# Eight experts on one core: six output stores moved into the load queue, a third output buffer, and a narrower last weight piece

## The chip, the cores and the metric

The kernel runs on one core of one Trainium2 chip. The metric is device time in microseconds for one execution of the whole program; lower is better.

## The reference

Each of 8 experts has its own 256 tokens and its own two-layer network; all tensors are float32 in HBM.

```python
n_experts, capacity, hidden, expert_hidden = 8, 256, 512, 2048
h = np.matmul(x, w1) + b1[:, np.newaxis, :]
h = np.maximum(h, 0)
out = np.matmul(h, w2) + b2[:, np.newaxis, :]
```

The weights are 4 MB per expert and per layer in float32. Every weight is used once, so 64 MB of weights have to come in from HBM for 8.6 GFLOP of matmuls.

## The kernel before

**Loads.** All weights and the tokens of experts 2 to 7 are loaded by DMAs that GpSimd issues, and they are cast from float32 to float16 on the way (`load_x`, `load_w1`, `load_w2`). All of them go into one DMA queue, called q0 in the profile; this text calls it the ring. `w1[e]` and `w2[e]` are one DMA of 2 MB (written) each. `w2[6]` is two DMAs of 1 MB. `w2[7]` is six pieces with a buffer each: rows 0 to 4, 4 to 8 and 8 to 12 of the 16 row blocks j (512 KB each), rows 12 to 14 (256 KB), and then rows 14 to 16 twice, once for the left and once for the right half of the 512 columns (128 KB each). The text names them p0, p4, p8, p12, p14a and p14b.

**Compute.** `first_product(e)` makes h for one expert: for each of 16 blocks j four matmuls (line 110) into PSUM, then a ReLU with bias on ScalarE (line 117) into `hT`. In the middle of it the tokens of the next expert are transposed on TensorE (`transposes`, line 97). `second_product(e)` starts with one bias matmul per accumulator (line 151), runs 32 matmuls of 512 columns (line 163) and calls `store`. For expert 7 the 512 columns are two blocks of `HH` = 256, and the pieces of `w2[7]` are used in the order in which they were loaded; the last two pieces give 4 matmuls each.

**Stores.** `store` copies the accumulator of token block 0 with VectorE (line 130) and that of token block 1 with ScalarE (line 131) to SBUF. For experts 0 to 6 SyncE then issues one DMA of 512 KB (line 137), which runs in another queue, q1 in the profile. For expert 7 each column block is stored by two DMAs, one issued by SyncE (line 134) and one by ScalarE (line 135).

**Order.** The main loop has 11 steps s. Step s runs `first_product(s)` and then `second_product(s - 3)`, so expert 0's second product comes after expert 3's first. TensorE's and GpSimd's instructions keep the order in which the program writes them. `issue_until` lets GpSimd run ahead: at step s it issues loads up to `w1[s + 2]` and `w2[s - 1]`. The three buffers each of `w1` and `w2` make the issue wait for the product that last read the buffer.

Of the kernel before, what the change touches and what calls it, by code (L numbers as in the profile page):

```python
# [11 lines left out]
def kernel(  # L12
# [9 lines left out]
    nc = tc.nc  # L22
    fp32 = mybir.dt.float32
    fp16 = mybir.dt.float16
    E, T, H = x.shape
    M = w1.shape[2]
    P = 128
    nTB = T // P
    nKC = H // P
    nJ = M // P  # L30
    HH = H // 2
    LAG = 3
    nXF32 = 2

    def ordered(ins):
        return tc.keep_in_program_order(ins)

    singles = ctx.enter_context(tc.tile_pool(name="singles", bufs=1))
    w1_pool = ctx.enter_context(tc.tile_pool(name="w1", bufs=3))
    w2_pool = ctx.enter_context(tc.tile_pool(name="w2", bufs=3))  # L40
    w2t_pool = ctx.enter_context(tc.tile_pool(name="w2t", bufs=1))
    x_pool = ctx.enter_context(tc.tile_pool(name="xp", bufs=4))
    xT_pool = ctx.enter_context(tc.tile_pool(name="xTp", bufs=2))
    hT_pool = ctx.enter_context(tc.tile_pool(name="hT", bufs=LAG + 2))
    out_pool = ctx.enter_context(tc.tile_pool(name="outp", bufs=2))
    psum_x = ctx.enter_context(tc.tile_pool(name="psum_x", bufs=1, space=bass.MemoryType.PSUM))
    psum_h = ctx.enter_context(tc.tile_pool(name="psum_h", bufs=3, space=bass.MemoryType.PSUM))
    psum_o = ctx.enter_context(tc.tile_pool(name="psum_o", bufs=2, space=bass.MemoryType.PSUM))
# [10 lines left out]
    w1_sb = [None] * E  # L59
    w2_sb = [None] * E  # L60
    hT = [None] * E

    def load_x(e):
        x16[e] = x_pool.tile([P, nTB, H], fp16, tag="x16", name="x16")
        ordered(nc.gpsimd.dma_start(  # L65
            out=x16[e], in_=x[e].rearrange("(p tb) h -> p tb h", tb=nTB)
        ))
# [7 lines left out]
    def load_w2(e):  # L75
        src = w2[e].rearrange("(p j) h -> p j h", j=nJ)
        w2_sb[e] = []
        if e < E - 1:
            t = w2_pool.tile([P, nJ, H], fp16, tag="w2", name="w2sb")
            step = nJ if e < E - 2 else nJ // 2  # L80
            for lo in range(0, nJ, step):
                ordered(nc.gpsimd.dma_start(out=t[:, lo : lo + step, :], in_=src[:, lo : lo + step, :]))  # L82
                w2_sb[e].append((lo, lo + step, 0, H, t[:, lo : lo + step, :]))
            return
        for lo, hi, c0, c1 in (
            (0, 4, 0, H), (4, 8, 0, H), (8, 12, 0, H), (12, 14, 0, H),
            (14, 16, 0, HH), (14, 16, HH, H),
        ):
            t = w2t_pool.tile([P, hi - lo, c1 - c0], fp16, tag=f"w2_{lo}_{c0}", name=f"w2_{lo}_{c0}")
            ordered(nc.gpsimd.dma_start(out=t, in_=src[:, lo:hi, c0:c1]))  # L90
            w2_sb[e].append((lo, hi, c0, c1, t))

    def transposes(e):
        pt = psum_x.tile([P, nKC, T], fp16, tag="psx", name="psx")
        for kc in range(nKC):
            for tb in range(nTB):
                ordered(nc.tensor.transpose(  # L97
                    out=pt[:, kc, tb * P : (tb + 1) * P],
                    in_=x16[e][:, tb, :].rearrange("p (q kc) -> p q kc", kc=nKC)[:, :, kc],
                    identity=ident16,  # L100
                ))
        xT[e] = xT_pool.tile([P, nKC, T], fp16, tag="xT", name="xT")
        nc.vector.tensor_copy(out=xT[e], in_=pt)  # L103

    def first_product(e):
        hT[e] = hT_pool.tile([P, nJ, T], fp16, tag="hT", name="hT")
        for j in range(nJ):
            ph = psum_h.tile([P, T], fp32, tag="ph", name="ph")
            for kc in range(nKC):
                ordered(nc.tensor.matmul(  # L110
                    out=ph,
                    lhsT=w1_sb[e][:, kc, :].rearrange("p (q j) -> p q j", j=nJ)[:, :, j],
                    rhs=xT[e][:, kc, :],
                    start=(kc == 0),
                    stop=(kc == nKC - 1),
                ))
            nc.scalar.activation(  # L117
                out=hT[e][:, j, :],
                in_=ph,
                func=mybir.ActivationFunctionType.Relu,  # L120
                bias=b1T[:, j, e : e + 1],
                scale=1.0,
            )
            if j == nJ // 2 and e + 1 < E:
                transposes(e + 1)

    def store(e, po, c0, c1, split):
        w = c1 - c0
        out_sb = out_pool.tile([P, nTB, w], fp32, tag=f"out{w}", name=f"out{w}")
        nc.vector.tensor_copy(out=out_sb[:, 0, :], in_=po[0])  # L130
        nc.scalar.copy(out=out_sb[:, 1, :], in_=po[1])  # L131
        dst = out[e].rearrange("(p tb) h -> p tb h", tb=nTB)[:, :, c0:c1]
        if split:
            nc.sync.dma_start(out=dst[:, 0, :], in_=out_sb[:, 0, :])
            nc.scalar.dma_start(out=dst[:, 1, :], in_=out_sb[:, 1, :])  # L135
        else:
            nc.sync.dma_start(out=dst, in_=out_sb)

    def second_product(e):
        if e < E - 1:  # L140
            blocks = [(0, H, psum_o, "po")]
        else:
            blocks = [(0, HH, psum_o, "po"), (HH, H, psum_h, "ph")]
        acc = {}
        for c0, c1, pool, tag in blocks:
            for tb in range(nTB):
                t = pool.tile(
                    [P, c1 - c0], fp32, tag=tag if tag == "ph" else f"{tag}{tb}", name=f"acc{tb}"
                )
                acc[c0, tb] = t  # L150
                ordered(nc.tensor.matmul(  # L151
                    out=t,
                    lhsT=ones1,
                    rhs=b2_sb[0:1, e * H + c0 : e * H + c1],
                    start=True,
                    stop=False,
                ))
        for lo, hi, p0, p1, t in w2_sb[e]:
            mine = [b for b in blocks if p0 <= b[0] and b[1] <= p1]
            for tb in range(nTB):  # L160
                for j in range(lo, hi):
                    for c0, c1, _, _ in mine:
                        ordered(nc.tensor.matmul(  # L163
                            out=acc[c0, tb],
                            lhsT=hT[e][:, j, tb * P : (tb + 1) * P],
                            rhs=t[:, j - lo, c0 - p0 : c1 - p0],
                            start=False,
                            stop=(j == nJ - 1),
                        ))
            if hi == nJ:  # L170
                for c0, c1, _, _ in mine:
                    store(e, [acc[c0, tb] for tb in range(nTB)], c0, c1, e == E - 1)

    x32 = singles.tile([P, nXF32, nTB, H], fp32)
    for e in range(nXF32):
# [4 lines left out]
        out=b2_sb,  # L180
        in_=b2.rearrange("e h -> (e h)").rearrange("(o f) -> o f", o=1),
# [10 lines left out]
    for j in range(nJ):  # L192
        for s in range(2):
            ordered(nc.tensor.matmul(  # L194
                out=pb[s * 64 : (s + 1) * 64, j, :, :],
# [5 lines left out]
    for s in range(2):  # L201
        nc.vector.tensor_copy(  # L202
            out=b1T[s * 64 : (s + 1) * 64, :, :], in_=pb[s * 64 : (s + 1) * 64, :, :, s]
        )
    transposes(0)

    loads = []
    for s in range(1, E + LAG):
        if s < E:
            if s >= nXF32:  # L210
                loads.append((load_x, s))
            loads.append((load_w1, s))
        if s >= LAG:
            loads.append((load_w2, s - LAG))
    n = 0

    def issue_until(done):
        nonlocal n
        while n < len(loads) and not done():
            loads[n][0](loads[n][1])  # L220
            n += 1

    for s in range(E + LAG):
        issue_until(lambda: (
            (min(s + 2, E - 1) < E and w1_sb[min(s + 2, E - 1)] is not None)
            and (s + 2 < LAG or w2_sb[min(s + 2 - LAG, E - 1)] is not None)
        ))
        if s < E:
            first_product(s)
        if s >= LAG:  # L230
            second_product(s - LAG)


# [28 lines left out]
```

## Time and profile before

| | |
|---|---|
| median of 5 runs | 185.95 us (185.87 to 186.2) |
| the profiled execution | 185.89 us, span 183.9 us (first to last instruction) |
| TensorE matmul busy | 139.2 us, 76% of the span |
| ScalarE busy | 62.7 us, 34% |
| VectorE, GpSimd busy | 13.4 us, 16.9 us |
| DMA queue q0 (the ring) | 35.14 MB written, 91.4% of the time of 16 DMA engines |
| DMA queue q1 (SyncE's) | 4.46 MB, 6.7% |
| HBM | 71.39 MB read, 4.19 MB written |
| granted TensorE clock, mean | 0.924 |

The span is 1.95 us shorter than the profiled execution's time, and that execution is 0.06 us under the median. Times inside the profile are microseconds from the start of the span. A DMA is complete when all 16 DMA engines have reported their share; the trace holds the time of each of the 16 reports, so a landing has a first, a mean and a last engine.

### The profile page before, as it was taken

The page shows a single profiled execution, that of the slowest core. Times are in us where ns is not written, and L with a number is a line of the kernel's source. Part 1 is how long each engine was busy: PE and PEld are TensorE (multiplying, and loading weights), DVE is VectorE, ACT ScalarE, POOL GpSimd, SP SyncE. Part 2 cuts the span into 40 slices and gives each one's busy share as a digit, 9 for nine tenths or more (in the row PEclk, how much of TensorE's full clock was granted, in tenths as well). Part 3 has the DMA queues.
Part 4 walks back from the last instruction along what each step waited for, and adds up shares of the span by engine and source line. Part 5 has one row for each costly group of instructions (what it writes and reads, how often), then busy time and mean ns, then how long its engine had stood idle before and what let it go on. Part 6 is the DMA issues. An engine that isn't in the chain of part 4 may idle for free.

```text
span 183.9 us, 2209 instructions
## 1 busy us (share of the span) xinstructions
PE 139.2 (76%) x946; PEld 99.3 (54%) x946; DVE 13.4 (7%) x22; ACT 62.7 (34%) x138; POOL 16.9 (9%) x37
## 2 busy tenths in 40 slices
PE   0556979399532999529996499926999994999991
PEld 0544979289522746527456364815649741434680
DVE  0320101001000101001010101001010010010101
ACT  0022879459540422704217150631509601010101
POOL 7100030300300011000110000100006100100000
PEclk9999999969996599975999879996999999699999
DMA  5999999999999999899999999999999999999993
GB/s 191 279 210 191 228 228 221 197 209 228 230 207 203 221 224 228 166 287 200 203 228 219 267 206 221 228 261 216 207 228 223 235 224 227 248 232 226 246 217 114
DMA packets 6488, 40.57 MB, mean 221 GB/s; under 512 B 688, under 2 KB 1728, under 8 KB 4432
## 3 DMA queue, kind: packets, MB, share of 16 engines
q0 software_dynamic: 4320, 35.14, 91.4%
q1 hardware_dynamic: 1568, 4.46, 6.7%
q10 hardware_dynamic: 592, 0.85, 1.3%
q8 instruction: 7, 0.11, 0.2%
q14 instruction: 1, 0.01, 0.0%
HBM read 71.39 MB, written 4.19 MB: 411 GB/s over the span
## 4 chain that ended last, share of the span: by engine, by line
DMA 83%; PE 12%; POOL 2%; issue 1%; ACT 0%; ACTq 0%; POOLq 0%
DMA w2sb<-in_w_dram 27%; DMA x<-in_x_dram 25%; DMA w<-in_w_dram 18%; DMA w1sb<-in_w_dram 12%; PE ph L110 7%; PE acc L163 4%; PE psx L97 1%; POOL w1sb L71 1%; ACT out L131 0%; PE acc L151 0%; POOL b_sb L179 0%; POOL w2sb L82 0%; POOL ident masks.py:199 0%; ACTq L135 0%; POOL ident masks.py:197 0%
## 5 line engine op out<-in xcount | busy, mean ns | idle before, releaser
L110 PE MATMUL ph<-xT,w1sb 128*128 128x256 f16 x512 | 68.8, 301 | 9.5 <-DMA w1sb<-in_w_dram 9.5
L117 ACT ACTIVATE hT<-ph,b1T 128x256 f16<-128x256 f32 x128 | 57.0, 474 | 45.9 <-PE ph L110 45.7
L110 PEld LDWEIGHTS <-w1sb 128*128 128x128 f16 x512 | 61.8, 149 | 15.8 <-DMA w1sb<-in_w_dram 10.5
L163 PE MATMUL acc<-w2sb,hT 128*128 128x512 f16 x224 | 51.1, 388 | 2.7 <-DMA w2sb<-in_w_dram 2.7
L163 PEld LDWEIGHTS <-hT 128*128 128x128 f16 x288 | 28.0, 99 | 33.0 <-issue 8.4
L131 ACT COPY out<-acc 128x512 f32<-128x512 f32 (+1 forms) x9 | 4.9, 542 | 61.0 <-PE acc L163 61.0
L97 PE MATMUL psx<-ident,x 128*128 128x128 f16 x64 | 6.6, 265 | 21.9 <-DMA x<-in_x_dram 21.2
L97 PEld LDWEIGHTS <-x 128*128 128x128 f16 x64 | 5.3, 128 | 22.9 <-DMA x<-in_x_dram 22.1
L103 DVE COPY xT<-psx 128x1024 f16<-128x1024 f16 x8 | 5.5, 691 | 83.1 <-PE psx L97 83.1
L130 DVE COPY out<-acc 128x512 f32<-128x512 f32 (+1 forms) x9 | 5.7, 632 | 74.9 <-PE acc L163 74.9
L71 POOL DMA_DIRECT2D w1sb<-in_w_dram x8 | 4.4, 553 | 69.7 <-PE ph L110 68.9
L82 POOL DMA_DIRECT2D w2sb<-in_w_dram x8 | 4.3, 536 | 55.5 <-PE acc L163 55.5
L194 PE MATMUL pb<-ident,b_rows 16*64 16x16 f32 x64 | 3.7, 266 | 6.9 <-DMA b_rows<-in_b_dram 6.9
L163 PE MATMUL acc<-w,hT 128*128 128x256 f16 x64 | 7.5, 273 | 0.1
L194 PEld LDWEIGHTS pb<-ident,b_rows 16*64 16x64 f32 x64 | 3.6, 198 | 6.8 <-issue 6.8
L117 ACT ACT_TABLE_LOAD x1 | 1.3, 1283 | 11.3 <-DVE b1T L202 11.3
L90 POOL DMA_DIRECT2D w<-in_w_dram x6 | 3.6, 614 | 13.8 <-DMA w2sb<-in_w_dram 13.8
L151 PE MATMUL acc<-b_sb,ones 1*128 1x512 f16 (+1 forms) x18 | 4.8, 355 | 0.0
L65 POOL DMA_DIRECT2D x<-in_x_dram x6 | 3.3, 546 | 0.8 <-DMA w1sb<-in_w_dram 0.8
L151 PEld LDWEIGHTS <-ones 1*128 1x128 f16 x18 | 1.1, 92 | 2.1 <-issue 2.1
L189 DVE CAST x<-x 128x1024 f16<-128x1024 f32 x2 | 1.5, 734 | 4.4 <-DMA x<-in_x_dram 4.4
L202 DVE COPY b1T<-pb 64x128 f32<-64x128 f32 x2 | 0.6, 288 | 3.7 <-PE pb L194 3.7
(8 smaller groups left out, 2.0 us busy)
## 6 DMA issues: line engine op xcount, KB each, us to landing
w1sb<-in_w_dram POOLq DMA_DIRECT2D x8, 2048.0 KB, 33.5
w2sb<-in_w_dram POOLq DMA_DIRECT2D x6, 2048.0 KB, 47.1
out_dram<-out SPq DMA_DIRECT2D x7, 512.0 KB, 8.7
w2sb<-in_w_dram POOLq DMA_DIRECT2D x2, 1024.0 KB, 25.6
x<-in_x_dram POOLq DMA_DIRECT2D x6, 256.0 KB, 40.2
w<-in_w_dram POOLq DMA_DIRECT2D x3, 512.0 KB, 33.2
x<-in_x_dram ACTq DMA_DIRECT2D x1, 512.0 KB, 5.4
x<-in_x_dram SPq DMA_DIRECT2D x1, 512.0 KB, 4.4
```

Source lines behind the costliest of these rows:

```text
L71: ordered(nc.gpsimd.dma_start(out=w1_sb[e], in_=w1[e].rearrange("(p kc) m -> p kc m", kc=nKC)))
L82: ordered(nc.gpsimd.dma_start(out=t[:, lo : lo + step, :], in_=src[:, lo : lo + step, :]))
L90: ordered(nc.gpsimd.dma_start(out=t, in_=src[:, lo:hi, c0:c1]))
L97: ordered(nc.tensor.transpose(out=pt[:, kc, tb * P : (tb + 1) * P], in_=x16[e][:, tb, :].rearrange("p (q kc) -> p q kc", kc=nKC)[:, :, kc] ...
L103: nc.vector.tensor_copy(out=xT[e], in_=pt)
L110: ordered(nc.tensor.matmul(out=ph, lhsT=w1_sb[e][:, kc, :].rearrange("p (q j) -> p q j", j=nJ)[:, :, j], rhs=xT[e][:, kc, :], start=(kc == 0),
L117: nc.scalar.activation(out=hT[e][:, j, :], in_=ph, func=mybir.ActivationFunctionType.Relu, bias=b1T[:, j, e : e + 1], scale=1.0,)
L130: nc.vector.tensor_copy(out=out_sb[:, 0, :], in_=po[0])
L131: nc.scalar.copy(out=out_sb[:, 1, :], in_=po[1])
L151: ordered(nc.tensor.matmul(out=t, lhsT=ones1, rhs=b2_sb[0:1, e * H + c0 : e * H + c1], start=True, stop=False,))
L163: ordered(nc.tensor.matmul(out=acc[c0, tb], lhsT=hT[e][:, j, tb * P : (tb + 1) * P], rhs=t[:, j - lo, c0 - p0 : c1 - p0], start=False, sto ...
L194: ordered(nc.tensor.matmul(out=pb[s * 64 : (s + 1) * 64, j, :, :], lhsT=b1_rows.rearrange("r (q j) -> r q j", j=nJ)[:, :, j], rhs=ident[0 ...
```

## The change

The stores of experts 0 to 5 (`e <= RING`) are no longer issued by SyncE. `store` leaves them in `pending`, and a new function `flush` issues them from GpSimd, in the ring, at fixed places between the loads. With that, the order of issue is written out in the list `ring`, whose entries have a step before which they are not issued. From the load of `w2[3]` on it reads: w2[3], store 0, x[7], w1[7], w2[4], store 1, w2[5], store 2, w2[6] in two halves, store 3, p0, store 4, p4, store 5, p8, p12, p14a, p14b. The output pool has three buffers in place of two. `HH` is 384 in place of 256, so p14a has 384 columns and p14b has 128, and expert 7's second product works on blocks of 384 and 128 columns. The store of expert 6 and those of expert 7 stay where they were.

```diff
-    HH = H // 2
+    HH = H - P
     LAG = 3
+    RING = 5
...
-    out_pool = ctx.enter_context(tc.tile_pool(name="outp", bufs=2))
+    out_pool = ctx.enter_context(tc.tile_pool(name="outp", bufs=3))
...
+    def flush(e):
+        dst, src = pending.pop(e)
+        ordered(nc.gpsimd.dma_start(out=dst, in_=src))
+
     def store(e, po, c0, c1, split):
         w = c1 - c0
-        out_sb = out_pool.tile([P, nTB, w], fp32, tag=f"out{w}", name=f"out{w}")
+        pool = out_pool if w == H else singles
+        out_sb = pool.tile([P, nTB, w], fp32, tag=f"out{c0}_{w}", name=f"out{w}")
...
+        elif e <= RING:
+            pending[e] = (dst, out_sb)
         else:
             nc.sync.dma_start(out=dst, in_=out_sb)
...
+    ring = []
+    for s in range(1, E + LAG - 1):
+        if s < E:
+            if s >= nXF32:
+                ring.append((s - 2, load_x, (s,)))
+            ring.append((s - 2, load_w1, (s,)))
+        if s >= LAG:
+            ring.append((s - 2, load_w2, (s - LAG,)))
+        if s >= 2 * LAG:
+            ring.append((s - 2, flush, (s - 2 * LAG,)))
+    e = E - LAG - 1
+    for piece in (
+        (0, 4, 0, H), (4, 8, 0, H), (8, 12, 0, H), (12, 14, 0, H),
+        (14, 16, 0, HH), (14, 16, HH, H),
+    ):
+        ring.append((0, load_w2_piece, (E - 1,) + piece))
+        if e <= RING:
+            ring.append((e + LAG + 1, flush, (e,)))
+            e += 1
 
     for s in range(E + LAG):
-        issue_until(lambda: (
-            (min(s + 2, E - 1) < E and w1_sb[min(s + 2, E - 1)] is not None)
-            and (s + 2 < LAG or w2_sb[min(s + 2 - LAG, E - 1)] is not None)
-        ))
+        while ring and ring[0][0] <= s:
+            _, put, args = ring.pop(0)
+            put(*args)
```

More of the change, by code (lines that the diff above doesn't have):

```diff
@@ L61 @@
     hT = [None] * E
+    pending = {}
     def load_x(e):
@@ L77, in load_w2, with load_w2_piece @@
         w2_sb[e] = []
[L78 to L91, printed above, removed]
+        t = w2_pool.tile([P, nJ, H], fp16, tag="w2", name="w2sb")
+        step = nJ if e < E - 2 else nJ // 2
+        for lo in range(0, nJ, step):
+            ordered(nc.gpsimd.dma_start(out=t[:, lo : lo + step, :], in_=src[:, lo : lo + step, :]))
+            w2_sb[e].append((lo, lo + step, 0, H, t[:, lo : lo + step, :]))
+    def load_w2_piece(e, lo, hi, c0, c1):
+        t = w2t_pool.tile([P, hi - lo, c1 - c0], fp16, tag=f"w2_{lo}_{c0}", name=f"w2_{lo}_{c0}")
+        src = w2[e].rearrange("(p j) h -> p j h", j=nJ)
+        ordered(nc.gpsimd.dma_start(out=t, in_=src[:, lo:hi, c0:c1]))
+        if w2_sb[e] is None:
+            w2_sb[e] = []
+        w2_sb[e].append((lo, hi, c0, c1, t))
     def transposes(e):
@@ L205 @@
     transposes(0)
-    loads = []
-    for s in range(1, E + LAG):
+    ring = []
+    for s in range(1, E + LAG - 1):
         if s < E:
             if s >= nXF32:
-                loads.append((load_x, s))
-            loads.append((load_w1, s))
+                ring.append((s - 2, load_x, (s,)))
+            ring.append((s - 2, load_w1, (s,)))
         if s >= LAG:
[L214 to L221, printed above, removed]
+            ring.append((s - 2, load_w2, (s - LAG,)))
[10 more added lines that the diff above has]
+            e += 1
     for s in range(E + LAG):
-        issue_until(lambda: (
-            (min(s + 2, E - 1) < E and w1_sb[min(s + 2, E - 1)] is not None)
-            and (s + 2 < LAG or w2_sb[min(s + 2 - LAG, E - 1)] is not None)
-        ))
+        while ring and ring[0][0] <= s:
+            _, put, args = ring.pop(0)
+            put(*args)
         if s < E:
@@ L231 @@
             second_product(s - LAG)
+    assert not ring and not pending
 _INS = ['x', 'w1', 'w2', 'b1', 'b2']
```

## The prediction

> **What bounds the kernel now.** I read the slices first, then the chain that ended last, TensorE's timeline near the end, the granted clock in short windows, and the 16 engines' reports of each DMA.
>
> The page's slices show the DMA engines full from the first slice to the last but one, with holes in TensorE and its clock:
>
> ```profile
> PE   0556979399532999529996499926999994999991
> ...
> PEclk9999999969996599975999879996999999699999
> DMA  5999999999999999899999999999999999999993
> ```
>
> The end of the chain of waits (start, length, what):
>
> ```profile
> 96.06 49.27 DMA w2sb<-in_w_dram
> 145.33 0.28 issue
> 145.61 33.35 DMA w<-in_w_dram
> 178.96 0.04 issue
> 179.00 0.61 PE acc L163 x4
> 179.62 0.02 issue
> 179.64 0.38 ACT out L131
> 180.02 0.02 issue
> 180.04 0.37 ACTq L135
> 180.41 0.04 issue
> 180.45 0.37 ACT out L131
> ```
>
> The ring's p14a lands at 178.96. Four matmuls, a ScalarE copy, ScalarE's DMA issue and a second copy follow in series; the last store then lands at 182.9, and the span ends at 183.94. p14b lands at 179.60 and is not on this chain: ScalarE is busy until 180.41.
>
> TensorE's timeline shows that TensorE, too, is barely in time:
>
> ```profile
> 155.99 8.66 PE L163 MATMUL acc<-w2sb,hT 128*128 128x512 f16 x32 [2.68 <-DMA w2sb<-in_w_dram]
> ...
> 165.11 7.08 PE L163 MATMUL acc<-w2sb,hT 128*128 128x512 f16 x32
> ...
> 172.67 7.58 PE L163 MATMUL acc<-w,hT 128*128 128x256 f16 x64
> ```
>
> Once `w2[5]` has landed (155.94), TensorE never waits until p14a. Its 56 matmuls on p0 to p12 run from 172.67 at 0.109 us each and end at 178.8, 0.2 us before p14a. So it is TensorE that keeps the pieces waiting, and not the other way round.
>
> Granted clock by windows of 3.41 us, laid on the trace's own clock changes (window, length, PE busy, clock, DMA share, GB/s):
>
> ```profile
> 97.81:101.22 3.41, 1.88 (x18) 1.00 0.94 228
> 101.22:104.63 3.41, 0.90 (x12) 1.00 1.26 296
> 104.63:108.04 3.41, 3.41 (x18) 0.50 0.91 196
> 118.29:121.70 3.41, 2.29 (x21) 1.00 0.92 208
> 152.42:155.83 3.41, 0.88 (x4) 1.00 0.91 190
> 155.83:159.24 3.41, 3.25 (x8) 0.50 1.02 243
> ```
>
> A window in which TensorE is busy for 0.90 us or less is followed by one at half clock; one with 1.88 us or more is not. That is why the second product of expert 5 took 8.66 us and that of expert 6 7.08.
>
> **Prices of the ring, from the reports.** Mean landing to mean landing, with no store in flight: 2 MB of weights 9.65 us, an x 1.25 (1.24 to 1.36). By bytes, half of `w2[6]` is 4.87, p0 like pieces 2.46, p12 1.26, p14a 0.65. With a store in flight the entries around store 1 took 9.81 + 2.32 + 9.87 = 22.00 where 2 x 9.65 + 1.25 = 20.55 was due; store 2 22.01 against 20.55; store 3 10.04 + 10.72 against 19.30. So a store in q1 costs the ring 1.45. Store 0 cost 2.1, because between 74 and 77 us packets of all engines took up to 1.97 us instead of 1.23; this 0.6 us follows SyncE's first store issue (73.05).
>
> **The moved stores.** In the ring a store is 8 packets of 4 KB per engine, at 172 ns in q1 now. An x load reads 4 KB per packet (173 ns) and costs 1.25, so I take 1.25. Bounds: 1.23 (8 x 0.154, the packets alone) and 1.45 (as in q1). Saving 0.2 per store, 0 to 0.22; for six, 0 to 1.3 (a loss would need a stall in each store, as store 0 had), plus 0.6 if store 0's stall goes too. Total bytes do not change, so that is all that the ring can gain. The larger effect is the order: stores 3 to 5 now stand between the last loads.
>
> Last-engine landings after the change (each 1.45 leaves, each 1.25 enters; 0.2 per store that stays ahead):
> - x[7]: now 125.57 behind stores 0 to 2; then behind store 0 alone: minus 2.9 minus 0.2 = 122.5.
> - `w2[5]`: 155.94 behind four; then two: minus 2.9 minus 0.4 = 152.6.
> - `w2[6]`: 166.99 behind five; then three: minus 2.9 minus 0.6 = 163.5.
> - p0: + 1.25 + 2.46 = 167.2. p4: + 1.25 + 2.46 = 170.9.
> - p8: + 1.25 + 2.46 = 174.6, and store 6 in q1 adds 1.4 (see below): 176.0.
> - p12: 177.3. p14a: 177.3 plus 1.5 x 0.65 = 178.3. p14b, half as wide: 178.6.
>
> **TensorE then.** From x[7] to the end of expert 4's second product it now runs 27.1 us without a wait (125.62 to 152.70); begun at 122.5 this ends at 149.6, and it waits for `w2[5]` until 152.6, as long as now. Expert 5 takes 8.6 again (or 7.3 at full clock), expert 6 7.4: end 167.3 to 168.6, against 172.1. The row before shows 172.1 to 172.89 for copies and store issue, and q1's first packets some 3 us after an issue. So store 6 moves packets from about 171.5 to 176, inside store 5 and p8. p0 is used up at 169.5 to 170.9 (16 x 0.109 = 1.75), p4 at 170.9 + 1.75 = 172.7. **TensorE then idles 3.3 us**, from 172.7 to 176.0, where it has no idle time now. After p8 there are 24 matmuls, 2.62 us: end 178.6, against p14a's 178.3. So TensorE is the last in the chain, and how fast its clock is decides.
>
> Idle 3.3 of a window of 3.41: if 2.5 us or more of it falls into one window, the row at 152.42 says that the clock halves; for a random position that is (3.41 + 3.3 - 2 x 2.5)/3.41 = 50%. In the other half the fullest window has 1.65 to 2.5 us of idle, between the rows with 0.90 and 1.88 busy, undecided; half of those give 75% in all. Price: at half clock for 3.41 us from somewhere between 175.0 and 177.5. From 175.0 the 2.62 us of work end at 179.8 (+1.2); from 176.0 at 180.3 (+1.7); from 177.5 it also doubles the last matmuls (+1.8). I take +1.5.
>
> The Trainium skill (TensorE: Matmul & The Clock Gate, "What's actually happening") says the same of idle windows of about 3.4 us, and adds that the window runs freely, so its position would differ between runs of one kernel. The runs before lie within 0.33 us, which shows no such spread. By the rule the two sums below, 185.9 and 187.3, would both be found among runs of the changed kernel; by the row either one.
>
> **The tail.** p14a has 384 columns: its four matmuls take 4 x 0.163 in place of 4 x 0.109, +0.2. ScalarE's copies (0.37 for 256 columns, 0.58 for 512) become 0.475 and 0.265: nothing in sum. p14b may land up to 1.1 us after p14a before it counts, since ScalarE copies and issues first (0.475 + 0.40) behind p14a's matmuls; its narrower transfer gains nothing, and more than 0.65 for it would be hidden as well. p14b's rows are 256 B in SBUF: the Trainium skill (DMA: Bandwidth & Descriptors, "Specifications") counts writes under 512 B as read-modify-write. No row here shows one that small; if it doubled 0.33 us, the sum would stay.
>
> **New waits.** GpSimd now waits for the copies before each moved store: some 0.4 to 1.1 us behind the second product's last matmul, plus 0.55 for the issue. Behind it stand x[7], w1[7], w2[5], w2[6] and the pieces. They land 20 to 50 us after their issue, so this is covered. The tightest is p8, held until expert 5's copies at about 162; the ring reaches it at 172. Without that cover each us of delay would be 1 us. The third output buffer frees copy 6 once store 3 has landed (164.8, needed at 168): nothing.
>
> **The sum.** At full clock: TensorE ready for p14a at 178.6 against 179.0 (-0.4), tail +0.2: about 0, span 183.7 to 183.9. With the half clock +1.5: 185.3. The profiled time is 1.95 above its span, the median 0.06 more: 187.3. Less than 0.2% (0.37 us) is what this measurement cannot tell from no change.
>
> **Rivals.**
> 1. *No half clock, the rest as above*: TensorE and ring cancel against the tail: 185.9 (185.6 to 186.3). For it: half of the window positions are undecided. Against it: the gap is longer than that at 152.9 to 155.99. Chance 0.16.
> 2. *Faster: the stall at 74 to 77 belongs to q1's first store and goes.* Every landing is then 0.6 earlier, p8 at 175.4, TensorE done at 178.0; without a half clock that is -1.0 + 0.2 from 185.95, or 185.15. It decides only where the gap before p8 stays under some 2.5 us in any window, since 1.5 outweighs 0.6; a store 6 that runs ahead of p8 would help. Speaks for it: no other store shows such packets. Against: it may be the first write to the output, whatever the queue. Chance 0.22, with ring stores at the cheap end.
> 3. *Ring stores as dear as in q1* (six x 0.2 = 1.2 later) on top of the half clock: 188.5. Chance 0.1 of the slower 0.62.
>
> Slower in all: 0.75 for the half clock, less what the gap may be shorter than worked out, 0.62. The range reaches from rival 2 (185.1) to between forecast and rival 3 (188.2).
>
> **What would show it.** Right: no L137 issue but one; the gap on TensorE before p8 of about 3 us near 173 to 176, behind a DMA; a half clock in the slices close to the end; matmuls of 128x384 at twice their pace there. Expert 6's second product ends near 168. Wrong: p8 lands soon after p4; or a clock of 1.00 from 170 on; or DMA landings of x[7] and `w2[5]` not 3 us earlier.

## The result and the profile after

The changed kernel takes 187.19 us in the median of 26 executions (185.98 to 188.8), the kernel before 186.15 (46 executions, 185.76 to 186.43). The ratio of the two is 1.0046, with a 95% interval of 1.0036 to 1.0057: that of the means (186.98 and 186.11), without the longest execution, 188.8. The medians alone give 1.0056. The prediction was 187.3, slower.

The executions of the changed kernel lie in two groups: nine from 185.98 to 186.56, one at 186.84, and sixteen from 187.07 upward. The first profile is of an execution like those of the first group: 186.28 us, span 184.5. Its page shows the DMA engines as full as before up to the last slice but one (6 in place of 9), and TensorE's last three slices at 6, 8 and 0 where they were 9, 9 and 1:

```profile
PE   0546999399631999469992999339999987999680
...
PEclk9999999969995799969998799956999997899997
DMA  5999999999999999999999999999999999999963
```

The end of its chain of waits:

```profile
163.09 0.53 POOL out_dram L130
163.62 12.49 DMA w<-in_w_dram
176.10 0.04 issue
176.15 2.86 PE acc L171 x24
179.01 0.00 issue
179.01 0.82 PE acc L171 x4
179.83 0.02 issue
179.85 0.65 ACT out L137 x2
```

Before, p14a's landing stood at the end of the chain. Now it is p8, issued at 163.62 right behind store 5 (163.09) and landed at 176.10; after it TensorE works through 24 and then 4 matmuls. TensorE's timeline has the gap that the prediction put there:

```profile
170.15 3.67 PE L171 MATMUL acc<-w,hT 128*128 128x384 f16 x32
176.15 3.90 PE L171 MATMUL acc<-w,hT 128*128 128x384 f16 x32 [2.33 <-DMA w<-in_w_dram]
```

In this execution the clock did not fall there. ScalarE's first copy for expert 7 starts at 179.85, against 179.64 before. The landings on the last engine, against the prediction's:

| | predicted | measured |
|---|---|---|
| x[7] | 122.5 | 123.02 |
| `w2[5]` | 152.6 | 153.33 |
| `w2[6]`, second half | 163.5 | 164.33 |
| p0, p4 | 167.2, 170.9 | 167.97, 171.74 |
| p8 | 176.0 | 176.10 |
| p12 | 177.3 | 177.93 |
| p14a, p14b | 178.3, 178.6 | 178.97, 179.32 |

### The profile page after: what moved, and what is told of

Same layout as the page of the kernel before. It is cut to its first block, busy times and chain, and to the rows that moved or that the text cites. A ratio compares the mean times of both kernels' runs of the same rounds, so it can differ in the third digit from the quotient of the medians.

```text
span 184.5 us, 2203 instructions
## 1 busy us (share of the span) xinstructions
PE 139.1 (75%) x946; PEld 98.2 (53%) x946; DVE 13.2 (7%) x22; ACT 62.6 (34%) x138; POOL 20.2 (11%) x43
## 4 chain that ended last, share of the span: by engine, by line
DMA 65%; PE 18%; issue 8%; another core or an unknown queue 3%; POOL 2%; ACT 1%; POOLq 0%; ACTq 0%
DMA x<-in_x_dram 24%; DMA w2sb<-in_w_dram 22%; DMA w1sb<-in_w_dram 12%; PE acc L171 11%; DMA w<-in_w_dram 7%; PE ph L111 6%; PE psx L98 1%; ACT out L137 1%; POOL out_dram L130 1%; POOL w2sb L83 1%; POOL w1sb L73 1%; PE acc L159 0%; POOL b_sb L187 0%; POOL ident masks.py:199 0%
## 5 line engine op out<-in xcount | busy, mean ns | idle before, releaser
L171 PEld LDWEIGHTS <-hT 128*128 128x128 f16 x288 | 26.8, 99 | 35.8 <-issue 9.6
L137 ACT COPY out<-acc 128x512 f32<-128x512 f32 (+2 forms) x9 | 4.8, 541 | 62.6 <-PE acc L171 62.6
L136 DVE COPY out<-acc 128x512 f32<-128x512 f32 (+2 forms) x9 | 5.6, 631 | 74.5 <-PE acc L171 74.5
L171 PE MATMUL acc<-w,hT 128*128 128x384 f16 (+1 forms) x64 | 7.6, 272 | 2.3 <-DMA w<-in_w_dram 2.3
L130 POOL DMA_DIRECT2D out_dram<-out x6 | 3.2, 539 | 29.8 <-ACT out L137 23.2
L159 PE MATMUL acc<-b_sb,ones 1*128 1x512 f16 (+2 forms) x18 | 4.8, 355 | 0.0
```

The costliest lines, as they stand in the source:

```text
L130: ordered(nc.gpsimd.dma_start(out=dst, in_=src))
L159: ordered(nc.tensor.matmul(out=t, lhsT=ones1, rhs=b2_sb[0:1, e * H + c0 : e * H + c1], start=True, stop=False,))
L171: ordered(nc.tensor.matmul(out=acc[c0, tb], lhsT=hT[e][:, j, tb * P : (tb + 1) * P], rhs=t[:, j - lo, c0 - p0 : c1 - p0], start=False, sto ...
```

## The experiments

Theory A is the prediction's: the moved stores open a gap on TensorE before p8, and in most executions the clock is halved for the matmuls after it. Theory B puts the cost on the narrow last piece p14b (and p14a, wider for it). Theory C says that the last pieces land later, whatever the clock.

**The slower group, profiled.** The changed kernel was run three more times with a profile.

> The changed kernel itself, profiled once more, since the profile at hand holds an execution of the quicker group. Theory A: where the execution takes 187 us or more, a half clock lies over the matmuls on p8 and p12 (24 matmuls in 4 us or more in place of 2.6 to 2.9), and the window of 3.41 us ahead of it has TensorE busy for under 1.4 us; where it takes under 186.7, there is none. Theory C: no such half clock in an execution of 187 us or more, but p14a landing 1 us later.

> As again1: another execution of the changed kernel, to see which group it falls into and whether the half clock goes with it.

> As again1: another execution of the changed kernel, to see which group it falls into and whether the half clock goes with it.

They took 187.62, 188.68 and 187.28 us, all of the slower group. The first one's timeline, from p0 on:

```profile
168.69 1.92 PE L171 MATMUL acc<-w,hT 128*128 128x384 f16 x16
172.02 1.91 PE L171 MATMUL acc<-w,hT 128*128 128x384 f16 x16 [1.40 <-DMA w<-in_w_dram]
176.94 4.98 PE L171 MATMUL acc<-w,hT 128*128 128x384 f16 x32 [3.02 <-DMA w<-in_w_dram]
```

and its clock by windows (window, length, PE busy with the number of instructions, clock, DMA share, GB/s):

```profile
169.43:172.84 3.41, 2.01 (x20) 1.00 1.05 298
172.85:176.26 3.41, 1.07 (x10) 1.00 1.06 271
176.26:179.67 3.41, 2.73 (x13) 0.50 0.70 102
```

The window with 1.07 us of work is followed by half clock, which lies over p8 and p12: the last 32 matmuls take 4.98 us in place of 3.90. In the third execution they take 5.32. The second one shows the most costly case, a half clock that stays for a second window:

```profile
172.08:175.49 3.41, 1.42 (x14) 1.00 1.05 281
175.49:178.90 3.41, 2.38 (x11) 0.50 0.89 138
178.91:182.32 3.41, 3.41 (x17) 0.50 0.01 2
```

There the 32 matmuls take 6.47 us. p14a landed at 179.18, 178.75 and 179.08 in these three, against 178.97 in the quick one. So Theory C falls: the landing is the same within 0.25 us, and the time differs by 1.0 to 2.4. The window ahead of the half clock had 1.42 us of work in the second execution, where under 1.4 was expected.

**The narrow piece alone.**

```diff
-    HH = H // 2
+    HH = H - P
```

> The kernel before with the last w2 pieces 384 and 128 columns wide in place of 256 and 256; stores as before. Theory A (the half clock in the gap that the moved stores open before p8): no gap before p8 here, so no spread; only the tail counts, p14a's four matmuls +0.2 us and p14a landing some 0.3 later, median 186.3 to 186.7, runs within 0.7 us of each other. Theory B (the narrow piece is what costs): median near the changed kernel's 187.2.

186.42 us (186.31 to 187.11, 12 executions) against 186.14, ratio 1.0018 (1.0008 to 1.0028); eleven of the twelve lie within 0.31, the twelfth makes the spread 0.80 where 0.7 was expected. So the narrow piece costs 0.28 us here and makes no second group. Theory B explains at most 0.28 of the 1.04 us.

**The stores alone.**

```diff
-    HH = H - P
+    HH = H // 2
```

> The changed kernel with the last w2 pieces 256 and 256 columns wide again; stores 0 to 5 stay in the ring. Theory A: two groups of times as in the changed kernel, about 185.8 to 186.3 and about 1 us and more above, median 186.8 to 187.1. Theory B: median at or under 186.2 and a spread under 0.7 us.

186.76 us (185.31 to 187.54), ratio 1.0018 (0.9997 to 1.0039): the median is 0.6 above before, but the interval does not exclude equality. The spread is 2.2 us where the kernel before has 0.75, and the profiled execution (186.9) has the half clock again:

```profile
175.93 5.32 PE L171 MATMUL acc<-w,hT 128*128 128x256 f16 x32 [2.62 <-DMA w<-in_w_dram]
```

The spread comes with the stores, as Theory A said; but the times run more evenly from 185.3 to 187.5 than in the two groups that were expected. The quickest, 185.31, is 0.45 under anything that the kernel before did. It was not profiled: that the stores in the ring are a gain without the half clock is likely by it, and not shown.

**The gap shortened without added work.** Store 5 goes behind p8.

```diff
-        if e <= RING:
+        if piece[0] in (0, 8):
             ring.append((e + LAG + 1, flush, (e,)))
```

> The changed kernel with store 5 behind p8 in the ring in place of ahead of it; all else as there, the same bytes ahead of p14a, no work added. The wait before p8 becomes 1.3 us shorter (about 1.1 in place of 2.3 in the profile), and as much waiting comes before p12. Theory A: no window is idle enough for the half clock, median 186.2 to 186.5, spread under 0.8 us. Theory C (p14a's landing alone decides): p14a lands when it did, median 187.2, spread as in the changed kernel.

186.22 us (185.95 to 186.58, 11 executions), ratio 1.0004 (0.9995 to 1.0013). The slower group is gone. p8 lands at 173.99 and p14a at 178.70; the waiting has split into 0.41 us before p8 and 1.79 before p12:

```profile
174.03 1.91 PE L171 MATMUL acc<-w,hT 128*128 128x384 f16 x16 [0.41 <-DMA w<-in_w_dram]
177.73 2.05 PE L171 MATMUL acc<-w,hT 128*128 128x384 f16 x16 [1.79 <-DMA w<-in_w_dram]
```

```profile
170.65:174.06 3.41, 3.00 (x29) 1.00 1.04 282
174.06:177.47 3.41, 1.87 (x16) 1.00 1.12 272
177.47:180.88 3.41, 2.05 (x16) 1.00 0.24 41
```

The emptiest window of the profiled execution has 1.87 us of work, and the clock stays at 1.00. The place of one store in the ring is worth 1 us of median here.

**The gap filled.** After p4's matmuls:

```diff
+            if e == E - 1 and lo == 4:
+                spare = psum_x.tile([P, H], fp32, tag="psx", name="spare")
+                for k in range(10):
+                    ordered(nc.tensor.matmul(
+                        out=spare, lhsT=hT[e][:, 4, 0:P], rhs=t[:, 0, :],
+                        start=(k == 0), stop=(k == 9),
+                    ))
```

> The changed kernel with ten matmuls of 512 columns on data that is already there, after p4's matmuls and before p8's; their result is not used. They add 2.2 us of TensorE work where it waits 2.3 us for p8 in the profile. Theory A: the slower group of times goes, median 186.2 to 186.5, spread under 0.8 us, and no half clock after 165 us in the profile. Theory C (data that lands later, whatever the clock): nothing gained, median 187.2 or above, spread as in the changed kernel.

186.29 us (185.94 to 187.41, 12 executions), ratio 1.0012 (0.9998 to 1.0025). Ten idle matmuls make the kernel 0.9 us quicker, and the profile has no half clock between 128 and 182 us. But two executions of twelve still took 186.92 and 187.41, so the spread is wider than expected. They were not profiled; what slowed them is open.

**Stores behind the last load.** The DMA engines are idle from p14b on, so the stores of experts 5 and 6 go there, both in the ring.

```diff
-    RING = 5
+    RING = 6
+    LATE = (5, 6)
...
-        if e <= RING:
+        if e <= 4:
             ring.append((e + LAG + 1, flush, (e,)))
             e += 1
+    for e in LATE:
+        ring.append((e + LAG + 1, flush, (e,)))
```

> The changed kernel with the stores of experts 5 and 6 in the ring behind p14b, where the 16 DMA engines are idle otherwise. Theory A and the ring's prices: between p4 and p8 now stand only p8's 2.5 us, so TensorE waits under 1 us there and the clock stays; the last pieces land 2.7 us earlier (1.27 and 1.4), p14a at about 176.4, TensorE at about 177; median 184.0 to 184.6, spread under 0.8 us. Theory C with stores that only change places: total bytes are equal, median 186 to 187.

183.52 us (183.32 to 183.58, 4 executions), ratio 0.9853 (0.9839 to 0.9868): better than both kernels and 0.5 better than expected. Its chain of waits ends 2.2 us earlier than in the changed kernel's first profile (the copies start at 177.62 in place of 179.85):

```profile
153.28 20.84 DMA w<-in_w_dram
174.11 0.04 issue
174.16 3.44 PE acc L172 x28
177.60 0.02 issue
177.62 0.65 ACT out L138 x2
```

p8 lands at 174.11 and TensorE waits 0.51 us for it. Stores 5 and 6 land at 178.03 and 179.28, while expert 7's copies and stores are under way, and ahead of the first landing of those stores (179.90; the last is 180.83). The profiled execution is 2.7 us quicker than that one (183.54 and 186.28); the other 0.5 us come after the copies: the last store lands 2.2 us after its issue, in the changed kernel's first profile 2.8, and the part on the price of the half clock, below, comes back to that.

**Further along that way.** Store 4 too (`LATE = (4, 5, 6)`); the late stores with 256 and 256 columns; and store 4 with filled time before expert 5.

> The changed kernel with the stores of experts 4, 5 and 6 in the ring behind p14b. Theory A and the ring's prices: another 1.27 us off the last loads, but TensorE, in late56 only 0.8 us of waits away from working without a pause from w2[5] on, becomes the bound: 182.7 to 183.2. If three stores behind the loads run into expert 7's own stores, 183.5 or above.

> late56 with the last pieces 256 and 256 wide again. Theory A: without a gap the narrow piece costs its tail only, 0.2 to 0.3 us, so 183.2 to 183.4 against 183.52. If the narrow piece pays where the loads are not the bound: 183.6 or above.

> late456 with eleven matmuls of 512 columns on data that is there, result not used, where TensorE waits 3.0 us for w2[5]. Theory A: the second product of expert 5 runs at full clock, 7.1 us in place of 8.5, and 1 us or more of that reaches the end before the loads are the bound again: 181.6 to 182.3. If the clock is not what makes expert 5 slow: 182.7 to 183.2 as late456.

They took 183.20 (ratio 0.9846, 0.9833 to 0.9860), 183.36 (0.9849, 0.9835 to 0.9862) and 183.19 us (0.9843, 0.9830 to 0.9857). The first two are within what was expected; all three intervals overlap late56's, so none is shown to be quicker than it. In late456 the copies do start 1.5 us earlier than in late56 (176.15), but three stores ahead of expert 7's own are more than the idle engines take without delay: the last store now takes 3.3 us from issue to landing (DMA issues from 176 on, first late56, then late456), so 0.4 us of the 1.5 are left.

```profile
out_dram<-out ACTq DMA_DIRECT2D x1, 64.0 KB, 2.2
...
out_dram<-out ACTq DMA_DIRECT2D x1, 64.0 KB, 3.3
```

The third is a miss: 181.6 to 182.3 was expected. Its profile has expert 5 at full clock, 7.07 us, but so has late456's, without the filled time. In both the last 28 matmuls start at p8's landing (173.08 and 172.64), so a quicker expert 5 only makes TensorE wait for p8: the loads were the bound already, where the expectation took 1 us or more to reach the end first.

## Why the prediction was right, point by point

**The gap and the half clock: right.** The gap before p8 was put at 3.3 us; it is 2.3 to 3.0 in the four profiles. It is longer (3.0) when expert 5 runs at full clock and TensorE is done with p4 earlier. The chance of a half clock in one execution was put at 75%, and that of a slower kernel at 62%; 16 of 26 executions are in the slower group, 62%, and one lies between. Only a profile tells which execution had the half clock: the three slower ones with a profile had it, the quick one had not. Both of the sums that the prediction gave, 185.9 and 187.3, have their group of executions. The undecided stretch, windows with 0.90 to 1.88 us of work, is now narrower: 1.42 us (again2) and 1.48 (the first profile, at 151.29) were followed by half clock, 1.55 and 1.75 (late456, at 52.34 and 151.33) were not.

**Its price: right, though the two groups differ by less.** The prediction took +1.5. The medians of the two groups are 186.32 and 187.33, a difference of only 1.0. But at expert 7's first copy on ScalarE the slower executions are behind the quick one by 1.88, 2.95 and 1.55 us (181.73, 182.80 and 181.40 against 179.85). The quick one loses 0.55 us of that again at its last store, which takes longer from issue to landing (DMA issues from 180.7 on, first the quick execution, then again3):

```profile
q14 instruction: 1, 0.01, 0.4%
out_dram<-out ACTq DMA_DIRECT2D x1, 64.0 KB, 2.8
...
q14 instruction: 1, 0.01, 0.3%
out_dram<-out ACTq DMA_DIRECT2D x1, 64.0 KB, 2.2
```

Fifteen engines report this store by 183.08 in the quick execution, the last at 183.59. Beside it stands an 8 KB packet of q14, which the profile lists as the queue of the instructions: it starts at 182.43, among the packets of the last stores. In the three slower executions it starts at 181.92 to 182.24, ahead of them, and the store lands 2.24 to 2.25 us after its issue. The profiles of shift5 and fill_gap have the packet among the stores and the late report too; the kernel before has no such packet near its end. That the packet is the cause was not tried, nor does a profile show the other quick executions; with 0.55 us for them too, the difference of the medians would be 1.55, near the +1.5.

**The no-half-clock case: 0.4 too low.** It was put at 185.9, and is 186.3. Half of that is the starting point: the prediction stood on the median of 5 executions before, 185.95, and the median of 46 is 186.15. Of the terms, "TensorE -0.4" is the one that failed. p14a was to land at 178.3 and TensorE to be ready at 178.6; p14a landed at 178.97, as late as before (178.96), and its matmuls start at 179.01 (before: 179.00). The ring was 0.84 late at p4 already, and store 6 moved its packets from 173.79 to 176.71, not from 171.5 to 176, so that it cost p12 as well as p8 time. The tail's +0.2 for the wider matmuls is there (0.82 us in place of 0.61). Two terms that were put at nothing are not: from the first copy to the last issue ScalarE takes 0.95 us in place of 1.21, and the last store lands 2.8 us after its issue in place of 2.1. So the +0.28 of hh_only is near the +0.2 without confirming it: in its profile p14a lands 0.36 later, and the same terms stand beside the matmuls.

**The sum: in part luck.** Its span was put at 185.3 us, and is 185.5 in again3, the slower execution nearest to the median. The time lies 1.76 us above the span there, in place of the 1.95 that was added. The misses of some 0.2 us cancel.

**The stores' price: nearly right.** Mean landing to mean landing, the six stores in the ring take 1.29, 1.29, 1.26, 1.35, 1.28 and 1.27, mean 1.29, where 1.25 was taken; in q1 it was 1.45. The saving of 1.0 us is there, and the landings show it, each within 0.9 of the prediction. Of the 0.5 us by which x[7] is late, 0.44 is there before any store: x[4] lands at 59.22 in this execution, at 58.78 in that of before. That is the last engine alone; the mean of the 16 reports is 58.03 and 57.97.

**Rival 2's stall: wrong in its cause.** It did not go with q1's first store. In the changed kernel packets of 1.4 to 1.84 us stand between 116.7 and 119 us, just ahead of the ring's first store; `w2[3]` takes 10.15 there in place of 9.65. The profiles of ring_only, shift5, late56 and late456 have it between 114 and 119 us as well, that of hh_only, whose stores are SyncE's, near 75. So in every profile looked at it goes with the first store, whatever the queue.

**New waits on GpSimd: right.** Store 5 is issued at 163.09 and p8 at 163.62, 9.4 us before the ring is done with store 5 (172.99).

## What to carry to other kernels

When a transfer is moved into a queue that is always full, its bytes cost nearly the same (here 1.29 us in place of 1.45); what changes is which wait it stands in front of, so list the landings behind it and the idle time that they open on the compute engine. A gap on TensorE can cost more than its length, if it empties a clock window before the last matmuls: two store positions with the same bytes ahead of the end differ by 1 us. The place for stores is where the DMA engines are idle, here behind the last load: with two of them there and the others in the ring the kernel is 2.6 us under the one before. A third one there delays the last stores (3.3 us to land in place of 2.2).

## What the runs showed of the hardware that was not expected

- Gaps on TensorE of 2.38 to 3.02 us before p8 were followed by the half clock, one of 2.33 us was not; a gap need not fill a window. In again2 the clock stayed halved for a second window after one with 2.38 us of work.
- The first store of the program is preceded by a stall of the DMA engines, in which packets take up to 1.84 us in the changed kernel (2.10 in again3) in place of 1.23, whichever queue the store is in. It costs half a microsecond; its cause was not tried.
- Rows of 256 B written to SBUF show no extra price: a packet takes 41 ns, after 60 ns for 512 B and 79 ns for 768 B, and p14b takes 0.37 us. The Trainium skill (DMA: Bandwidth & Descriptors, "Specifications") puts line rate at transfers of 512 B or more and says that the DMA does read-modify-write below that; no such cost is seen in these loads, and the measured times stand.
